# Two layers of a GLA, MLA and S5 hybrid: where S5 coefficients and powers are computed, how much filling goes where, and which PSUM banks GLA's decays use

## The chip, the cores and the metric

The kernel runs on one core of one Trainium2 chip. The metric is the device time of one execution in microseconds; the median of three runs is given. TensorE is called PE (PEld is its weight load), VectorE DVE, ScalarE ACT, GpSimd POOL; SP is the engine that issues the DMAs.

## The reference, cut to what matters

Two layers are computed for 512 latent tokens and 128 context tokens together (640 columns). Each layer normalises and modulates its input, projects it, runs three branches and merges them with sigmoid gates before an output projection:

```python
h = rms_norm(x, p['norm_w']) * (1.0 + scale) + shift
(gq, gk, gv, gaf, gab, g_gate, mq, mkv, mkr, m_gate, su, s_gate, merge) = split_cols(h @ p['w_in'], IN_SPLITS)
o_a = gla_mixer(...)      # gated linear attention, chunks of 64 tokens, both directions
o_b = mla_mixer(...)      # latent attention, 4 heads
o_c = s5_mixer(...)       # diagonal state space, both directions
g_a, g_b, g_c = jnp.split(jax.nn.sigmoid(merge), 3, axis=-1)
mixed = g_a * (o_a @ w_bo_gla) + g_b * (o_b @ w_bo_mla) + g_c * (o_c @ w_bo_s5)   # each o gated by silu
y = x + gate * (mixed @ p['w_out'])
```

Two pieces matter here. S5 needs coefficients that depend on weights alone (`s5_discretise`: exponentials, a sine and a cosine, a complex division) and the powers of the discretised transition; its linear scan is done in blocks. In GLA, each chunk of 64 tokens needs the cumulated decay `bcum`, from it three exponentials, and the addition `einsum('bhcd,bhce->bhde', kr, vi)` to the state that is carried from chunk to chunk.

## The kernel before, in words

**Layout and stages.** Activations stand with channels on partitions and the 640 tokens along the free axis. A projection takes 128 x 512 pieces of weights from DRAM (`raw`, tile `wraw`), splits each into a rounded high part on ACT (`whi`, line 227) and a remainder on DVE (`wlo`, line 236), and multiplies them with the split activations, all through one helper (line 245). Each layer goes in order through: the inputs of S5 (`s5_su`, `s5_kernel`, `s5_in`, `s5_z`), the S5 scan (`s5_pow`, `s5_scan`), S5's output (`s5_y`, `s5_gelu`), its gated linear unit (`s5_glu`), MLA (`mla_qkv`, `mla_heads`), GLA (`gla_in`, `gla_heads`), the last merge and the output projection.

**Filling.** The order of PE's instructions is the order in which the program writes them; all other engines are ordered by a scheduler with priorities (`high_priority`, a larger number is earlier) against a simulated timeline. Between its own steps a stage calls `fill(n)`, which takes n steps from a list of standing projections, `self.stand`: a step is one 128-row slice of a projection, six matmuls of 128 x 320. A projection from `h` has eight such steps. The list holds `mla_raw` (18 projections: S5 gates, MLA's latents, the output gates), then `mer_early` (8 merge gates, parked in DRAM), and after `s5_glu` also the merge of S5's branch. `settle` steps on to the end of the current projection; `fill(1000)` at the end of MLA drains what stands there. How many steps go where is set by `FILL` (S5, and MLA's inputs), `FM` (MLA's heads) and `FG` (GLA):

```python
FILL = (17, 2, 1, 4, 2, 10, 10, 1, 7, 3)
FM = (1, 6, 1, 4, 2, 4, 3, 2, 1)
```

`FILL[3]` is used after each of the 4 doublings of `s5_pow` and of the scan's steps, `FILL[4]` and `FILL[9]` in each of the four calls of `s5_y`, `FILL[5]` ahead of the gated linear unit.

**S5's coefficients.** `s5_prep` loads B and C (lines 636 to 641), and computes on DVE, in some 110 small instructions (lines 600 to 709), the powers `s5pw`, the weights `s5w` and the block transition `s5ab`. For layer 0 this is done at the start; for layer 1 by `s5_open(1)`, ahead of layer 0's last merge. `s5_kernel` then forms from them the tables `s5qk` (lines 716 to 718), and PE multiplies these in the course of layer 0's output projection.

**S5's powers.** `s5_pow` (lines 861 to 875) forms the powers 1 to 16 of the block transition (`s5pt`) by four doublings, just ahead of the scan that uses them (lines 896 to 934).

**PSUM.** The tiles `pj` (two of two banks) serve projections; four single banks (`bank`) serve all else. In `gla_head` the decays of a head are multiplied into two banks `pb` (the matmuls named `bank<-c,la`), and read by DVE (lines 1351, 1352) and ACT (`kd`, `eb`). The chunk additions (`bank<-gvt,krt`) go into four banks: chunk pair 4 into two, pairs 0 to 3 into two more; DVE reads pair 4 in lines 1403, 1404 and in the two `fin` updates of line 1400, and then the rest in the chain of `st` updates of the same line. `gla_heads` has the parts of neighbouring heads interleaved: the additions of head h are followed on PE by the decays of head h+1, then by eight steps of filling, then by the output of head h.

**Pools.** Tiles of a stage come from pools that are opened and closed like a stack; a tile that takes the place of another waits for the last use of that tile. `s5_in` and `s5_z` share one pool. The pools of MLA are opened right after the one of `s5_glu` is closed; MLA's keys `kt` are first written by ACT.

Of the kernel before, what the change touches and what calls it, by code (L numbers as in the profile page):

```python
# [10 lines left out]
F32 = mybir.dt.float32  # L11
# [8 lines left out]
L = 2  # L20
# [161 lines left out]
    return {k: np.ascontiguousarray(v) for k, v in r.items()}, at  # L182


FILL = (17, 2, 1, 4, 2, 10, 10, 1, 7, 3)
FM = (1, 6, 1, 4, 2, 4, 3, 2, 1)
FG = (8, 4, 8, 6)
TCARGS = dict(schedule_with_timeline_sim=True)
# [13 lines left out]
class Prog:  # L202
# [16 lines left out]
    def pool(self, name, bufs=1, **kw):  # L219
        return self.es.enter_context(self.tc.tile_pool(name=name, bufs=bufs, **kw))  # L220
# [95 lines left out]
    def consts(self):  # L316
        nc, a = self.nc, self.a
        c = self.cst.tile([128, 660], F32, name="c")
        self.S.dma_start(c, a["cst"])
        self.ident, self.trif, self.trib = (c[:, 128 * i:128 * i + 128] for i in range(3))  # L320
        self.eye16 = c[:, 384:400]
        self.rope = c[:, 400:656].rearrange("p (t r x) -> p t r x", t=4, r=2)
        self.sgn, self.nsgn, self.mhalf, self.one = (c[:, 656 + i:657 + i] for i in range(4))
        m = self.cst.tile([128, 2, 64], U32, name="msk")
        self.S.dma_start(m, a["msk"].rearrange("p (a b) -> p a b", a=2))
        self.msk = m
        cr, ct = (self.th.tile([128, NT], F32, name="tmp", tag="tmp", bufs=2)[:, 0:16].rearrange("p (a b) -> p a b", b=2)
                  for _ in range(2))
        self.S.dma_start(cr, a["cond"])
        self.act(ct, cr, AF.Tanh, scale=0.5)  # L330
        self.V.tensor_scalar(ct, ct, 0.5, 0.5, op0=ALU.mult, op1=ALU.add)
        cp = self.cst.tile([128, 8, 32], F32, name="cond")
        self.V.memset(cp, 0.0)
        self.V.tensor_tensor(cp[:, :, 0:2], ct, cr, op=ALU.mult)
        self.cond = cp
        self.kd = [self.dr.tile([16, 32, 240], F32, name=f"kd{l}") for l in range(L)]
        self.qd = [self.dr.tile([8, 2, 128, 512], F32, name=f"qd{l}") for l in range(L)]
        self.sud = [self.dr.tile([NT, 512], F32, name=f"sud{l}") for l in range(L)]
        self.gd = [self.dr.tile([8, 128, NT], F32, name=f"gd{l}") for l in range(L)]
        self.md = [self.dr.tile([8, 128, NT], F32, name=f"md{l}") for l in range(L)]  # L340
        self.x1 = self.dr.tile([8, 128, NT], F32, name="x1")

    def vecs(self, l):
# [285 lines left out]
        V.tensor_copy(e, k)  # L629
        V.tensor_tensor(out, y, e.bitcast(F32), op=ALU.mult)  # L630

    def s5_prep(self, l, vec, p, pz, ptmp):

        V = self.V
        n0 = VEC["B1"][0]
        bs, cs = pz.tile([128, 1024], F32, name="s5b"), p.tile([128, 1024], F32, name="s5c")
        with self.tc.high_priority(5200):
            for i, t in enumerate((bs, cs)):
                self.S.dma_start(t, self.a["vec"][l][:, n0 + 1024 * i:n0 + 1024 * i + 1024])
        self.B1, self.B2, self.C1, self.C2 = (t[:, 512 * i:512 * i + 512].rearrange("p (g c) -> p g c", c=16)  # L640
                                              for t in (bs, cs) for i in range(2))
        are, aim, ldt = vec("are"), vec("aim"), vec("ldt")
        sm = ptmp.tile([128, 11, 64], F32, name="s5sm")
        dt, tre, th, kk = (sm[:, i] for i in range(4))
# [29 lines left out]
        V.tensor_tensor(cs, c0, aq, op=ALU.mult)  # L674
        V.tensor_tensor(x2, s0, q, op=ALU.mult)
        V.tensor_tensor(cs, cs, x2, op=ALU.subtract)
        pw = p.tile([128, 9, 2, 64], F32, name="s5pw")
        V.memset(pw[:, 0, 0, :], 1.0)
        V.memset(pw[:, 0, 1, :], 0.0)
        V.tensor_tensor(pw[:, 1, 0], tre, cs, op=ALU.mult)  # L680
# [15 lines left out]
        e = lambda lo, hi, i: pw[:, lo:hi, i]  # L696
        for lo, hi, f in ((2, 3, 1), (3, 5, 2), (5, 9, 4)):
            n = hi - lo
            br, bi = (pw[:, f, i][:, None, :].to_broadcast([128, n, 64]) for i in range(2))
            self.cmul(V, ptmp, e(lo, hi, 0), e(lo, hi, 1), e(1, 1 + n, 0), e(1, 1 + n, 1), br, bi, [128, n, 64])  # L700
        w = pz.tile([128, 8, 2, 64], F32, name="s5w")
        br, bi = (t[:, None, :].to_broadcast([128, 8, 64]) for t in (cr, ci))
        self.cmul(V, ptmp, w[:, :, 0], w[:, :, 1], e(0, 8, 0), e(0, 8, 1), br, bi, [128, 8, 64])
        V.tensor_scalar(w[:, :, 1], w[:, :, 1], self.sgn, None, op0=ALU.mult)
        ab = p.tile([128, 2, 64], F32, name="s5ab")
        V.tensor_copy(ab[:, 0], pw[:, 8, 0])
        V.tensor_scalar(ab[:, 1], pw[:, 8, 1], self.nsgn, None, op0=ALU.mult)
        V.tensor_scalar(pw[:, 1:9, 0], pw[:, 1:9, 0], self.nsgn, None, op0=ALU.mult)
        V.tensor_scalar(pw[:, 1:9, 1], pw[:, 1:9, 1], -1.0, None, op0=ALU.mult)
        self.pw, self.w, self.ab = pw, w, ab  # L710

    def outer(self, eng, p, out, tmp, s1, s2, m1, m2, shape):

# [612 lines left out]
    def gla_head(self, p, h):  # L1326

        V, T, l = self.V, self.T, self.l
        v = self.gv
# [4 lines left out]
            self.copy(q[ds], self.gq[h // 2][hs])  # L1334
            self.copy(k[ds], self.gk[h // 2][hs])
        tri = (self.trif, self.trib)
        pb = [self.bank(), self.bank()]
        for t in range(5):
            for d in range(2):
                o = pb[t // 4][64 * d:64 * d + 64, 128 * (t % 4):128 * (t % 4) + 128]  # L1340
                self.mm(o, self.la[:, t, 128 * h + 64 * d:128 * h + 64 * d + 64], tri[d], tile_position=(0, 64 * d))
        big = lambda nm, b: p.tile([128, NT], F32, name=nm, tag=nm, bufs=b)
        eb, kd, kr = big("eb", 1), big("kd", 1), big("kr", 1)
        bl = p.tile([128, 10], F32, name="bl", tag="bl", bufs=2)
        for ps, c, n in ((pb[0], slice(0, 512), 8), (pb[1], slice(512, 640), 2)):
            src = ps[:, 0:64 * n]
            for d in range(2):
                s3 = src[64 * d:64 * d + 64].rearrange("p (c x) -> p c x", x=64)
                end = s3[:, :, 63:64] if d == 0 else s3[:, :, 0:1]
                e = bl[64 * d:64 * d + 64, c.start // 64:c.start // 64 + n]  # L1350
                V.tensor_copy(e, end[:, :, 0])
                V.tensor_tensor(kr[64 * d:64 * d + 64, c].rearrange("p (c x) -> p c x", x=64),
                                e[:, :, None].to_broadcast([64, n, 64]), s3, op=ALU.subtract)
            self.act(kd[:, c], src, AF.Exp, scale=-1.0)
            self.act(eb[:, c], src, AF.Exp)
# [8 lines left out]
        krt = p.tile([128, 5, 128], F32, name="krt", tag="krt", bufs=1)  # L1364
        for t0, nt in ((0, 4), (4, 1)):
            ps = self.bank()
# [5 lines left out]
        ps = [self.bank(), self.bank()]  # L1372
        for t in range(5):
            for d in range(2):
                for j in range(2):
                    c = slice(128 * t + 64 * j, 128 * t + 64 * j + 64)
                    self.mm(ps[d][64 * j:64 * j + 64, 64 * t:64 * t + 64], kd[64 * d:64 * d + 64, c], qd[64 * d:64 * d + 64, c],
                            tile_position=(64 * d, 64 * j))
# [8 lines left out]
        f, b = slice(0, 64), slice(64, 128)  # L1387
        self.S.dma_start(st[f, 0, :], self.a["sgla"][l, h, 0:64])
        self.S.dma_start(st[b, 7, :], self.a["sgla"][l, h, 64:128])
        pu = {}  # L1390
        for ts in ((4,), range(4)):
            ps = [self.bank(), self.bank()]
            for t in ts:
                for j in range(2):
                    r = slice(64 * j, 64 * j + 64)
                    pu[2 * t + j] = ps[j][:, 128 * (t % 4):128 * (t % 4) + 128]
                    self.mm(pu[2 * t + j], krt[r, t, :], v[r, t, 128 * h:128 * h + 128], tile_position=(64 * j, 0))

        def upd(r, out, c):
            V.scalar_tensor_tensor(out, st[r, c, :], bl[r, c:c + 1], pu[c][r], op0=ALU.mult, op1=ALU.add)  # L1400
# [12 lines left out]
        g = self.gate_in(4 + h)  # L1413
# [3 lines left out]
        ps = [self.bank(), self.bank()]  # L1417
        o = [ps[t // 4][:, 128 * (t % 4):128 * (t % 4) + 128] for t in range(5)]
# [18 lines left out]
        for t0, nt in ((0, 4), (4, 1)):  # L1437
            ps = self.bank()
            for t in range(t0, t0 + nt):
                T.transpose(ps[:, 128 * (t - t0):128 * (t - t0) + 128], on[:, t, :], self.ident)  # L1440
            c = slice(128 * t0, 128 * (t0 + nt))
# [24 lines left out]
    def fill(self, n):  # L1466

        for _ in range(n):
            while self.stand:
                try:  # L1470
                    next(self.stand[0])
                    break
                except StopIteration:
                    self.stand.pop(0)
# [14 lines left out]
    def s5_open(self, l):  # L1489

        es, ek = ExitStack(), ExitStack()
        pa = es.enter_context(self.pool_("s5a", l))
        pz = ek.enter_context(self.pool_("s5w", l))
        vec = self.nvec if l else self.vec
        with self.pool_("s5p", l) as p:
            self.s5_prep(l, vec, pa, pz, p)
        pk = ExitStack()
        self.s5 = es, ek, pk, pa, pz, self.s5_kernel(l, vec, pk.enter_context(self.pool_("s5k", l)))

    def layer(self, l, x):  # L1500
        tc = self.tc
        self.l = l
        self.layer_vecs()
        pool = lambda n, **kw: self.pool_(n, l, **kw)
        run = lambda g: [None for _ in g]
        step = lambda g, n: [next(g, None) for _ in range(n)]
        fill = self.fill
# [5 lines left out]
        if l == 0:  # L1513
# [8 lines left out]
            g = pair(0, 8000)  # L1522
            both(g, 2)
            n = self.h_rstd()
# [5 lines left out]
        else:  # L1530
            g = self.h_rstd()
# [9 lines left out]
        es, ek, pk, pa, pz, kern = self.s5  # L1541
# [24 lines left out]
            fill(2)  # L1566
        pk.close()
        self.late_vecs()
        with pool("s5i") as p, tc.high_priority(2000):
            self.s5_in(pa, p, fill)  # L1570
            self.s5_z(p, fill)
        ek.close()
        with ExitStack() as eg:
            with es:
                pq = es.enter_context(pool("s5q"))
                with pool("s5s") as p:
                    for _ in self.s5_pow(p):
                        fill(FILL[3])
                    for _ in self.s5_scan(p):
                        fill(FILL[3])  # L1580
                pg = eg.enter_context(pool("s5g", side="right"))
                gl = []
                with pool("s5y") as p:
                    for cb in range(4):
                        with tc.high_priority(2000):
                            y = self.s5_y(pq, p, cb, fill)
                        gl.append(self.s5_gelu(pg, y))
            with pool("s5b") as p:
                ogc = self.s5_glu(p, gl, self.gates, fill)
        self.stand = [g for g in self.stand if g is not early] + [  # L1590
            self.finish_tile(early), self.alternate(self.merge(2, ogc, 0), self.ada(l, self.vec, 2)), early]
# [62 lines left out]
```

## Time and profile before

| | |
|---|---|
| median of 3 runs | 1593.46 us (1589.63 to 1594.63) |
| the profiled execution | 1595.56 us, its span 1593.8 us |
| PE busy | 1517.0 us (95%) |
| DVE busy | 1051.9 us (66%) |
| ACT busy | 629.6 us (40%) |
| POOL busy | 48.0 us (3%) |
| TensorE clock granted, mean | 0.981 of full speed |

An engine is busy while one of its instructions runs. PE's busy time counts the whole length of matmuls that overlap, so what a matmul costs in a row of them is read from the distance of their starts. The chain of work that ended last follows the last instruction back through what released each step; PE has 87% of it. A granted clock below 1 in a stretch is a mean of the two levels 1.2 and 2.4 GHz.

### The profile page before, as it was taken

To read this page: it belongs to the slowest core of one execution; us is meant where nothing else is said; L and a number is where in the kernel's file an instruction comes from. 1 tells how busy PE (TensorE), PEld (TensorE's weight loads), DVE (VectorE), ACT (ScalarE), POOL (GpSimd) and SP (SyncE) were. 2 spreads that over 40 slices of the span, in tenths; PEclk is the share of its full clock that TensorE was granted. 3 is DMA by queue.
4 is the path that set the end of the run, shared out by engine and by line. 5 is a ranking of instruction groups with operands and counts; after the bars stand their busy time and mean duration, and the time that the engine had idled before them with its cause. 6 is when DMAs were issued, how large, how long until landed. Compare 5 with 4: busy or idle time off the path is not lost.

```text
span 1593.8 us, 28777 instructions
## 1 busy us (share of the span) xinstructions
PE 1517.0 (95%) x11334; PEld 1442.5 (91%) x11334; DVE 1051.9 (66%) x2435; ACT 629.6 (40%) x1171; POOL 48.0 (3%) x48
## 2 busy tenths in 40 slices
PE   5999999999999799999799999999999988999999
PEld 3789999999998688898797999999989988888998
DVE  8976993357666436879987579724766663487662
ACT  3335222545444355323223542244544443633331
POOL 0000000012000000000000000000210000000000
PEclk9999999999999899999999999999999999999999
DMA  9451435323321121227663432452333122222353
GB/s 348 156 150 50 142 122 155 119 86 113 116 61 52 46 76 52 68 90 242 216 202 90 124 113 90 130 160 77 100 119 95 62 66 66 64 65 62 93 168 106
DMA packets 108792, 179.73 MB, mean 113 GB/s; under 512 B 12656, under 2 KB 30768, under 8 KB 108656
## 3 DMA queue, kind: packets, MB, share of 16 engines
q1 hardware_dynamic: 108656, 177.89, 35.8%
q8 instruction: 89, 1.46, 0.4%
q14 instruction: 47, 0.39, 0.1%
HBM read 149.23 MB, written 28.61 MB: 112 GB/s over the span
## 4 chain that ended last, share of the span: by engine, by line
PE 87%; DVE 7%; DMA 3%; ACT 2%; issue 1%; SPq 0%; POOL 0%; DVEq 0%; ACTq 0%
PE pj L245 64%; PE bank L245 19%; PE bank L1236 2%; DMA wraw<-wpk 1%; PE bank L825 1%; DVE wlo L236 1%; ACT P L230 1%; DMA s5cr<-sud 1%; PE bank L1183 0%; DVE gt L418 0%; DVE smx L1211 0%; ACT whi L227 0%; DVE og L236 0%; DVE P L1222 0%; DVE mx L456 0%
## 5 line engine op out<-in xcount | busy, mean ns | idle before, releaser
L245 PE MATMUL pj<-h,whi 128*128 128x320 f32 x3456 | 662.8, 313 | 0.0
L245 PEld LDWEIGHTS pj<-h,whi 128*128 128x128 f32 x3456 | 541.2, 189 | 6.0 <-issue 5.1
L227 ACT ACTIVATE whi<-wraw 128x512 fp32r<-128x512 f32 x326 | 204.7, 631 | 502.0 <-PE pj L245 368.4
L245 PE MATMUL pj<-h,wlo 128*128 128x320 f32 x1728 | 397.4, 310 | 0.0
L236 DVE TENSOR_TENSOR wlo<-wraw,whi 128x512 fp32r<-128x512 f32 x326 | 223.5, 687 | 255.5 <-ACT whi L227 249.2
L245 PEld LDWEIGHTS pj<-h,wlo 128*128 128x128 f32 x1728 | 290.3, 188 | 0.0
L245 PE MATMUL pj<-og,whi 128*128 128x320 f32 x736 | 141.9, 313 | 1.0 <-DVE og L236 1.0
L245 PEld LDWEIGHTS pj<-og,whi 128*128 128x128 f32 x736 | 114.8, 188 | 5.0 <-issue 1.9
L245 PE MATMUL pj<-whi,h 128*128 128x512 f32 x256 | 87.0, 401 | 5.1 <-ACT h L230 4.4
L245 PE MATMUL pj<-og,wlo 128*128 128x320 f32 x384 | 87.5, 309 | 0.0
L245 PEld LDWEIGHTS pj<-whi,h 128*128 128x128 f32 x256 | 48.6, 192 | 18.3 <-ACT h L230 5.1
L245 PEld LDWEIGHTS pj<-og,wlo 128*128 128x128 f32 x384 | 64.2, 188 | 0.0
L230 ACT ACTIVATE P<-bank,smx 128x384 f32<-128x384 f32 x64 | 36.4, 575 | 56.3 <-DVE smx L1215 56.3
L236 DVE TENSOR_TENSOR Ptl<-bank,Pth 128x512 fp32r<-128x512 f32 x48 | 32.1, 688 | 35.5 <-ACT Pth L227 35.0
L230 ACT ACTIVATE th<-pj 128x640 f32<-128x640 f32 x72 | 49.7, 690 | 6.0 <-PE pj L245 6.0
L245 PE MATMUL pj<-wlo,h 128*128 128x512 f32 x128 | 50.7, 396 | 0.0
L245 PE MATMUL pj<-s5g,whi 128*128 128x320 f32 x256 | 49.2, 315 | 0.0
L245 PE MATMUL bank<-s5qy,mx 128*80 128x128 f32 x256 | 46.1, 302 | 0.0
L1236 PE MATMUL bank<-c,P 128*128 128x128 f32 x192 | 33.6, 315 | 12.8 <-ACT P L230 5.3
L227 ACT ACTIVATE Pth<-bank 128x512 fp32r<-128x512 f32 x48 | 27.5, 597 | 42.5 <-PE bank L1236 42.5
L1211 DVE TENSOR_REDUCE smx<-bank 128x1 f32<-128x384 f32 (+1 forms) x72 | 36.2, 523 | 9.4 <-PE bank L245 8.6
L245 PEld LDWEIGHTS pj<-s5g,whi 128*128 128x128 f32 x256 | 41.2, 193 | 0.0
(349 smaller groups left out, 2327.5 us busy)
## 6 DMA issues: line engine op xcount, KB each, us to landing
wraw<-wpk SPq DMA_DIRECT2D x358, 256.0 KB, 2.9
og<-wpk SPq DMA_DIRECT2D x48, 256.0 KB, 5.1
qd<-s5qk SPq DMA_DIRECT2D x32, 256.0 KB, 2.2
s5qy<-qd SPq DMA_DIRECT2D x32, 256.0 KB, 3.9
gd<-gt SPq DMA_DIRECT2D x16, 320.0 KB, 2.6
gt<-gd SPq DMA_DIRECT2D x16, 320.0 KB, 3.1
md<-th SPq DMA_DIRECT2D x16, 320.0 KB, 2.3
th<-md SPq DMA_DIRECT2D x16, 320.0 KB, 3.2
```

The source lines that it names most:

```text
L227: self.A.activation(out, in_, AF.Copy, scale=scale)
L230: self.A.activation(out, in_, f, **kw)
L236: (eng or self.V).tensor_tensor(lo, src, hi.bitcast(F32), op=ALU.subtract)
L245: self.T.matmul(out, lhsT, rhs, start=start, stop=stop, skip_group_check=True, **kw)
L825: self.T.transpose(ps[:, 128 * i:128 * i + 128], r[:, i].rearrange("p a b -> p (a b)"), self.ident)
L1211: V.tensor_reduce(mx[:, i:i + 1], ps[:, 0:w], axis=AX.X, op=ALU.max)
L1236: self.T.transpose(pt[:, nq * i + 128 * qi:nq * i + 128 * qi + 128], pr[qi][:, 128 * k:128 * k + 128], self.ident)
```

## The change

The diff, cut to its core:

```diff
-FILL = (17, 2, 1, 4, 2, 10, 10, 1, 7, 3)
+FILL = (17, 2, 1, 4, 1, 4, 10, 1, 7, 1)
+PREP = 200
+POW = 300
+        self.cd = self.dr.tile([128, 2304], F32, name="cd")
...
-    def s5_prep(self, l, vec, p, pz, ptmp):
+    def s5_prep(self, l, vec, p, pz):
...
+        self.pw = p.tile([128, 9, 2, 64], F32, name="s5pw")
+        self.w = pz.tile([128, 8, 2, 64], F32, name="s5w")
+        self.ab = p.tile([128, 2, 64], F32, name="s5ab")
+        if l:
+            for t, a, n in ((self.pw, 0, 9), (self.w, 1152, 8)):
+                self.S.dma_start(t, self.cd[:, a:a + 128 * n].rearrange("p (e r g) -> p e r g", r=2, g=64))
+            self.S.dma_start(self.ab, self.cd[:, 2176:2304].rearrange("p (r g) -> p r g", r=2))
+        else:
+            with self.pool_("s5p", l) as ptmp:
+                self.s5_coef(vec, self.pw, self.w, self.ab, ptmp)
+
+    def s5_coef_ahead(self, vec, p):
+        pw, w = p.tile([128, 9, 2, 64], F32, name="s5pw"), p.tile([128, 8, 2, 64], F32, name="s5w")
+        ab = p.tile([128, 2, 64], F32, name="s5ab")
+        self.s5_coef(vec, pw, w, ab, p)
+        for t, a, n in ((pw, 0, 9), (w, 1152, 8)):
+            self.S.dma_start(self.cd[:, a:a + 128 * n].rearrange("p (e r g) -> p e r g", r=2, g=64), t)
+        self.S.dma_start(self.cd[:, 2176:2304].rearrange("p (r g) -> p r g", r=2), ab)
+
+    def s5_coef(self, vec, pw, w, ab, ptmp):
...
-        pb = [self.bank(), self.bank()]
+        pb = self.rest if h else [self.bank(), self.bank()]
         for t in range(5):
             for d in range(2):
-                o = pb[t // 4][64 * d:64 * d + 64, 128 * (t % 4):128 * (t % 4) + 128]
+                o = pb[t // 3][64 * d:64 * d + 64, 128 * (t % 3):128 * (t % 3) + 128]
...
-        for ps, c, n in ((pb[0], slice(0, 512), 8), (pb[1], slice(512, 640), 2)):
+        for ps, c, n in ((pb[0], slice(0, 384), 6), (pb[1], slice(384, 640), 4)):
...
-        for ts in ((4,), range(4)):
-            ps = [self.bank(), self.bank()]
-            for t in ts:
-                for j in range(2):
-                    pu[2 * t + j] = ps[j][:, 128 * (t % 4):128 * (t % 4) + 128]
+        self.rest = [self.bank(), self.bank()]
+        ps = [self.bank(), self.bank()]
+        for t in (4, 0, 1, 2, 3):
+            for j in range(2):
+                pu[2 * t + j] = self.rest[j][:, 384:512] if t == 4 else ps[j][:, 128 * t:128 * t + 128]
...
-        with pool("s5i") as p, tc.high_priority(2000):
-            self.s5_in(pa, p, fill)
-            self.s5_z(p, fill)
+        with tc.high_priority(2000):
+            with pool("s5i") as p:
+                self.s5_in(pa, p, fill)
+            ep = ExitStack()
+            pt = ep.enter_context(pool("s5t", side="right"))
+            with tc.high_priority(-POW):
+                for _ in self.s5_pow(pt):
+                    pass
+            with pool("s5z") as p:
+                self.s5_z(p, fill)
...
                 with pool("s5s") as p:
-                    for _ in self.s5_pow(p):
-                        fill(FILL[3])
                     for _ in self.s5_scan(p):
                         fill(FILL[3])
+                ep.close()
...
-            with pool("s5b") as p:
+            with pool("s5b") as p, pool("s5f") as pf:
+                if l + 1 < L:
+                    with tc.high_priority(-PREP):
+                        self.s5_coef_ahead(self.nvec, pf)
                 ogc = self.s5_glu(p, gl, self.gates, fill)
```

So layer 1's coefficients are computed in layer 0 beside the gated linear unit, at a lowered priority, stored to DRAM (`cd`) and loaded again by `s5_open(1)`. The powers are written ahead of `s5_z`, with no filling between their doublings. `s5_y` gets 1 step of filling in each of two places where it had 2 and 3, the gated linear unit 4 where it had 10. In GLA, the additions of chunk pair 4 and the decays of the next head stand in the same two banks, in different columns.

## Rows read from the trace of the kernel before

**Rows 1.** Windows of 20 us: length, busy us (count) by engine, PE clock, DMA share, GB/s
```profile
340.00:360.00 20.00, 20.00 (x147) 19.16 (x146) 14.45 (x30) 11.75 (x23) 2.01 (x2) 1.00 0.36 105
...
520.00:540.00 20.00, 12.39 (x59) 10.56 (x60) 12.34 (x33) 8.83 (x24) 0.00 (x0) 0.73 0.06 23
...
780.00:800.00 20.00, 10.89 (x87) 10.25 (x86) 19.76 (x36) 3.75 (x6) 0.00 (x0) 0.80 0.55 187
```

**Rows 2.** Who waited for whom, PE: us in total, times, longest us
```profile
PE bank L245 <- DVE s5qk L718: 12.2, 4, 9.1
PE bank L245 <- DVE fin L1400: 9.0, 6, 2.1
```

**Rows 3.** The chain that ended last, by time: start us, us, what
```profile
160.52 100.35 PE pj L245 x684
260.87 6.21 PE bank L245 x48
...
303.84 17.64 PE pj L245 x120
```

**Rows 4.** Windows: the matmuls of `pj` alone in one MLA head
```profile
460.50:499.40 38.90, 28.43 (x177) 25.93 (x176) 1.64 (x2) 1.40 (x2) 1.00 0.21 63
```

**Rows 5.** PE's timeline: last filling in MLA's heads, first projection after them, both layers
```profile
501.71 0.75 PE L245 MATMUL pj<-h,whi 128*128 128x320 f32 x4
...
544.13 0.83 PE L245 MATMUL pj<-h,whi 128*128 128x320 f32 x4
...
1299.05 0.74 PE L245 MATMUL pj<-h,whi 128*128 128x320 f32 x4
...
1326.68 0.83 PE L245 MATMUL pj<-h,whi 128*128 128x320 f32 x4
```

**Rows 6.** Timeline of DVE and ACT: end of the scan; S5's output and its gelu
```profile
244.46 0.65 DVE L934 TENSOR_TENSOR mx<-mx,sf 128x480 f32<-128x480 f32 x1
...
267.12 0.59 ACT L227 ACTIVATE s5yb<-bank 80x512 f32<-80x512 f32 x1 [2.51 <-PE bank L245]
...
309.27 0.82 DVE L236 TENSOR_TENSOR s5g<-og,s5g 128x640 fp32r<-128x640 f32 x1 [0.30 <-ACT s5g L227]
```

**Rows 7.** ACT's last `s5cg`, and PE's first transposes of `s5_z`
```profile
123.26 1.06 ACT L227 ACTIVATE s5cg<-s5cr 80x1024 f32<-80x1024 f32 x1 [0.87 <-DMA s5cr<-sud]
...
124.98 0.60 PE L825 MATMUL bank<-c,s5r 128*128 128x128 f32 x4
```

**Rows 8.** Windows by tile: DVE's `ex`, `s5sm`, `cm` (coefficients), then `sp` (powers)
```profile
708.00:778.00 70.00, 8.63 (x44) 1.00 0.66 218
...
708.00:778.00 70.00, 12.32 (x61) 1.00 0.66 218
...
708.00:778.00 70.00, 9.09 (x24) 1.00 0.66 218
...
158.00:186.00 28.00, 9.10 (x24) 1.00 0.56 159
```

**Rows 9.** The chain that ended last, layer 0's output projection
```profile
796.59 2.69 PE bank L245 x26
799.28 8.63 PE pj L245 x48
807.91 1.47 PE bank L245 x26
```

**Rows 10.** Window of the gated linear unit, and ACT's first `kt`
```profile
303.84:323.61 19.77, 19.77 (x142) 19.77 (x141) 9.59 (x15) 10.22 (x17) 0.84 (x1) 1.00 0.32 102
...
354.39 0.38 ACT L227 ACTIVATE kt<-bank 128x256 f32<-128x256 f32 x1
```

**Rows 11.** GLA's timeline at one head change: DVE, PE, then ACT
```profile
618.29 0.72 DVE L1400 SCALAR_TENSOR_TENSOR fin<-st,bl,bank 64x128 f32<-64x128 f32 x2
...
618.77 1.31 PE L245 MATMUL bank<-c,la 128*64 128x128 f32 x20 [2.10 <-DVE fin L1400]
...
624.77 0.60 ACT L230 ACTIVATE kd<-bank 128x512 f32<-128x512 f32 x1 [8.99 <-DVE kr L1352]
```

More of the change, by code (lines that the diff above doesn't have):

```diff
@@ L630, in exp_ @@
         V.tensor_tensor(out, y, e.bitcast(F32), op=ALU.mult)
-    def s5_prep(self, l, vec, p, pz, ptmp):
-        V = self.V
+    def s5_prep(self, l, vec, p, pz):
         n0 = VEC["B1"][0]
@@ L641, in s5_prep @@
                                               for t in (bs, cs) for i in range(2))
+        self.pw = p.tile([128, 9, 2, 64], F32, name="s5pw")
[16 more added lines that the diff above has]
+    def s5_coef(self, vec, pw, w, ab, ptmp):
+        V = self.V
         are, aim, ldt = vec("are"), vec("aim"), vec("ldt")
@@ L676, in s5_prep @@
         V.tensor_tensor(cs, cs, x2, op=ALU.subtract)
-        pw = p.tile([128, 9, 2, 64], F32, name="s5pw")
         V.memset(pw[:, 0, 0, :], 1.0)
@@ L700, in s5_prep @@
             self.cmul(V, ptmp, e(lo, hi, 0), e(lo, hi, 1), e(1, 1 + n, 0), e(1, 1 + n, 1), br, bi, [128, n, 64])
-        w = pz.tile([128, 8, 2, 64], F32, name="s5w")
         br, bi = (t[:, None, :].to_broadcast([128, 8, 64]) for t in (cr, ci))
@@ L704, in s5_prep @@
         V.tensor_scalar(w[:, :, 1], w[:, :, 1], self.sgn, None, op0=ALU.mult)
-        ab = p.tile([128, 2, 64], F32, name="s5ab")
         V.tensor_copy(ab[:, 0], pw[:, 8, 0])
@@ L709, in s5_prep @@
         V.tensor_scalar(pw[:, 1:9, 1], pw[:, 1:9, 1], -1.0, None, op0=ALU.mult)
-        self.pw, self.w, self.ab = pw, w, ab
     def outer(self, eng, p, out, tmp, s1, s2, m1, m2, shape):
@@ L1390, in gla_head @@
         pu = {}
-        for ts in ((4,), range(4)):
-            ps = [self.bank(), self.bank()]
-            for t in ts:
-                for j in range(2):
-                    r = slice(64 * j, 64 * j + 64)
-                    pu[2 * t + j] = ps[j][:, 128 * (t % 4):128 * (t % 4) + 128]
-                    self.mm(pu[2 * t + j], krt[r, t, :], v[r, t, 128 * h:128 * h + 128], tile_position=(64 * j, 0))
+        self.rest = [self.bank(), self.bank()]
+        ps = [self.bank(), self.bank()]
+        for t in (4, 0, 1, 2, 3):
+            for j in range(2):
+                r = slice(64 * j, 64 * j + 64)
+                pu[2 * t + j] = self.rest[j][:, 384:512] if t == 4 else ps[j][:, 128 * t:128 * t + 128]
+                self.mm(pu[2 * t + j], krt[r, t, :], v[r, t, 128 * h:128 * h + 128], tile_position=(64 * j, 0))
         def upd(r, out, c):
@@ L1494, in s5_open @@
         vec = self.nvec if l else self.vec
-        with self.pool_("s5p", l) as p:
-            self.s5_prep(l, vec, pa, pz, p)
+        self.s5_prep(l, vec, pa, pz)
         pk = ExitStack()
```

## The prediction

> **What bounds the kernel now.** The table comes first: PE is busy for 1517.0 of 1593.8 us, so all that any reordering can win is the 77 us in which PE stands, and the time that it works at a lower clock. No matmul is removed. I therefore looked for the holes in PE with windows of 20 us: most are full, and some are not [rows 1]: 520 to 540 has PE busy for 12.39 us at a mean clock of 0.73 (part of it at 1.2 instead of 2.4 GHz), 780 to 800 for 10.89 us at 0.80. The list of PE's waits names what ends two kinds of hole: DVE's `s5qk` (12.2 us, one wait of 9.1) and `fin` (9.0 us in six waits) [rows 2]. The chain shows the opposite, stretches of S5 that are filling and nothing else: 100.35 us of `pj` beside the scan [rows 3]. The rest was read from timelines of those stretches.
>
> **Filling moved from S5 to MLA.** 684 matmuls in 100.35 us are 0.147 us each, so a step of six takes 0.88 us [rows 3]. Per layer 4 x 4 steps go from the powers, 4 x (1 + 2) from S5's output, 6 from ahead of the gated linear unit: 34. Ahead of that unit `settle` ends a projection: 120 matmuls stand there before, 20 steps, of which 8 are its own first projection and 10 `FILL[5]`, so 2 are `settle`'s [rows 3]; with 34 fewer it takes 4. Net 32 steps, 28.2 us, arrive in MLA.
>
> MLA runs out of them now. In layer 0 the last step starts at 501.71 and the next projection at 544.13; in layer 1 at 1299.05 and 1326.68 [rows 5]. From the ends of those steps that is 41.5 and 26.8 us. What PE must do there without filling: a full head takes 38.90 us with 177 matmuls of filling [rows 4], 26.0 us at 0.147, and the other 12.9 us hold by the code 101 matmuls, 0.128 each. Counted from the code, 142 such remain in layer 0 (from the second half of head 2's second score block) and 83 in layer 1 (in head 3): 18.2 and 10.6 us. So 23.3 and 16.2 us are latency and low clock. The steps that the code asks for in those stretches and does not get are 42 and 26, some 0.55 to 0.63 us lost for each. With 32 more, layer 1 is covered (16.2 us); layer 0 lacks 10, which keep about 6 us: 17.3 us. **Together -33.5 us**; none (0) if S5 turns out to need them all.
>
> Does S5 need them? The scan's last DVE instruction ends at 245.1 [rows 6], its first consumer on PE starts at 260.87 [rows 3]. 16 steps fewer bring that to 246.8; the powers, 24 small and medium instructions of 9.1 us together [rows 8], leave the scan too, so it ends at about 237. Covered, by 9 us. If the powers didn't fit ahead, cover would still be 1.6 us. In S5's output the last product of a block ends at 260.87 + 6.21 = 267.08, ACT's copy at 267.71 [rows 3, 6]; one step of 0.88 us covers all of it, a release may add some 0.2 us. Eight blocks: **+1.5 us**, between 0 and 8 x 2.64 = 21 (the three removed steps all idle). The gelu's last product is ready at 310.1 [rows 6], 6.3 us after the filling starts at 303.84 [rows 3]; the eight steps that stay last 7.0, and it is needed as the fourth slice, 2.6 us later. Covered.
>
> **Powers ahead of `s5_z`.** They run at a lower priority in DVE's idle time. The pool is split, so `s5_z`'s first tiles take the places of `s5cr` and `s5cg` and wait for their last uses. The last `s5cg` copy ends at 124.3; two DVE steps of 0.6 us each put the first transposes at about 125.6 in place of 124.98 [rows 7]: **+0.6 us a layer, +1.2**, between 0 and 4.
>
> **Layer 1's coefficients.** `ex`, `s5sm` and `cm` have 8.6, 12.3 and 9.1 us on DVE between 708 and 778 [rows 8]; some of it counts twice, 20 to 28 us is the load. DVE is full when PE waits 9.1 us for `s5qk` [rows 1, 2]. With that load gone, the tables (some 8 us for the first) are early and the wait goes. The 48 matmuls behind it took 8.63 us [rows 9] against 7.04 at 0.147: 1.6 us of low clock go with it. **-10.7 us**, or 0 if DVE's queue is still late. What is late next: the loads of the powers and weights, which the first table then waits for.
>
> Added: three stores to `cd` and three loads, 1.18 MB each way, on SP's queue. The loads fall in a stretch where DMA is at 0.55 to 0.66 of its time [rows 1, 8], with the weights' loads behind them: **+1 us**, 0 to 4. The computation itself lies beside the gated linear unit, where DVE is busy 9.59 of 19.77 us [rows 10] and then 14.45 of 20 [rows 1]: at these two rates 19 to 26 us are free until ACT writes the first `kt` at 354.39 [rows 10], about what the coefficients need. `kt` comes from a pool that takes over the place of the coefficients, so it waits for them and for the store; a few microseconds may show: **+2 us**, 0 to 8.
>
> **GLA's banks.** PE waits for `fin` ahead of the decays [rows 2, 11]: their new banks are those of chunk pair 4, free after DVE's reads. In the new form they are the same banks by construction, and other columns. If only columns counted, the 9.0 us would go. But ACT's `kd` stood 8.99 us until DVE's `kr` [rows 11]: neither reads what the other writes, they read one bank. I conclude that users of one bank are ordered whatever the columns, so the decays still stand behind `fin`, and behind the second one, since the first bank is the one that it reads: 0.72 / 2 = 0.36 us more for each of six [rows 11]: **+2.2 us**, between -9 and +2.2.
>
> The Trainium skill (PSUM — Partial Sum Buffer, on PSUM bank collisions) says that two engines must not use one bank in the same 32-partition quadrant at once, disjoint columns included, and that accesses are therefore serialised. By that rule the edit wins nothing, which the row of `kd` bears out; without it the sum would be 11 us lower.
>
> **The sum.** -33.5 + 1.5 + 1.2 - 10.7 + 1 + 2 + 2.2 = -36.3 us. From the profiled execution, 1595.56, that is 1559.3; it stands 2.1 us above the median of the runs, so I predict **1557 us**.
>
> **Rivals.** *S5 cannot spare its filling.* For: PE never waits there now, so its true slack is not seen, and each block's copy ends just when one step does. Against: the ends read above. All 21 us in place of 1.5: 1577.
>
> *DVE stays late at `s5qk`.* For: DVE has 19.76 of 20 us there [rows 1], some of it merge and projection work. Against: 20 us or more leave. 10.7 us come back: 1568.
>
> *Columns count in GLA*, and PE's decays go at once. Against: the `kd` row. 11 us less, and the state updates give a little back: 1547.
>
> *Slower: `kt` behind the coefficients.* Their lowered priority lets DVE's MLA work go first; then only about 5.5 of each 20 us are free [rows 1], and 25 us of work left over would stretch past 420. ACT is in order: with `kt` waiting, weight splits behind it stand, and PE with them. From 354 to past 400, less what PE has in hand, is 35 to 50 us, about 1597. It decides from 36 us on, where the whole gain is gone. Against: DVE is half idle for 40 us before, and the priority is lowered by 200 instructions only.
>
> **The numbers.** The forecast has 0.52, S5 short of filling 0.14, `s5qk` still late 0.12, columns in GLA 0.10, `kt` late 0.12. The range: the two nearer rivals and most of the first lie between 1545 and 1577, and the forecast's own unknowns (21, 4, 8, 4 us upwards, mostly not together) too; that leaves out the slow case and an edge of the others: 1543 to 1579. 0.3% (4.8 us) is about what a measurement of this kernel can tell from no change. Only the last rival reaches it: 0.05 within, 0.07 slower, 0.88 faster.
>
> **What would show it.** Right: no hole at 500 to 545 and 1300 to 1327 but for a short one in layer 0, head 3; the chain's stretch beside the scan near 86 us; no long wait on `s5qk`; `fin` still among PE's waits with about 9 to 11 us. Wrong: PE waiting for `s5yb`, for the scan or for `s5r` in S5; ACT's `kt` waiting for DVE or a store in layer 0; SP standing at a `cd` transfer while ACT waits for `wraw`; `fin` gone.

## The result and the profile after

The changed kernel takes **1575.01 us** (median of 6 runs, 1573.82 to 1577.47) against 1593.3 for the kernel before (6 runs): ratio 0.9892, 95% interval 0.9877 to 0.9906. It is 18.3 us faster by the medians, 17.2 by the ratio: inside the forecast range, with about half of the forecast gain of 36 us. The profiled execution takes 1574.24 us, its span is 1572.5 us, its mean granted clock 0.986 (0.981 before).

Windows of the changed kernel, columns as in [rows 1]:

```profile
120.00:140.00 20.00, 12.87 (x88) 12.36 (x87) 17.10 (x30) 7.26 (x14) 0.00 (x0) 0.74 0.18 57
...
340.00:360.00 20.00, 19.41 (x107) 17.10 (x108) 15.17 (x67) 9.67 (x20) 6.79 (x7) 0.91 0.32 103
520.00:540.00 20.00, 17.03 (x102) 15.77 (x100) 11.98 (x31) 8.73 (x20) 0.00 (x0) 0.83 0.25 77
720.00:740.00 20.00, 17.70 (x128) 14.76 (x129) 20.00 (x31) 4.64 (x8) 0.00 (x0) 1.00 0.91 293
780.00:800.00 20.00, 20.00 (x179) 19.27 (x178) 14.35 (x28) 5.65 (x10) 0.00 (x0) 1.00 0.57 193
880.00:900.00 20.00, 12.71 (x92) 12.27 (x90) 13.97 (x23) 8.09 (x15) 0.00 (x0) 0.83 0.16 44
1300.00:1320.00 20.00, 20.00 (x138) 20.00 (x137) 5.55 (x8) 6.21 (x10) 0.06 (x1) 1.00 0.38 119
```

The two holes of [rows 1] have moved. 780 to 800 is full, 520 to 540 has PE busy for 17.03 us in place of 12.39, and layer 1's MLA is full. Two new holes stand at 120 and 880, 7.1 and 7.3 us of idle PE, at 0.74 and 0.83 of the clock. They are in `s5_z` of the two layers. The list of PE's waits over the whole span names them (us in total, times, longest; lines of the helpers are two higher than before, `s5r` is line 738):

```profile
PE bank L845 <- DVE s5r L738: 11.4, 2, 6.1
PE bank L247 <- DVE fin L1421: 10.7, 6, 2.4
...
PE bank L247 <- DVE s5qk L738: 3.2, 3, 1.4
...
PE pj L247 <- DVE og L238: 2.4, 3, 1.4
PE bank L247 <- ACT kt L229: 2.4, 1, 2.4
```

Against [rows 2], `s5qk` fell from 12.2 to 3.2 us (what is left is layer 0's start), `fin` rose from 9.0 to 10.7, `og` from 1.0 to 2.4, and `s5r` is new. The wait for `og` lies at the last merge of layer 0, from 720 on, where DVE is busy for all of the 20 us.

PE's timeline at the last filling of MLA in layer 0, for [rows 5]:

```profile
528.83 0.75 PE L247 MATMUL pj<-h,whi 128*128 128x320 f32 x4
...
540.67 0.83 PE L247 MATMUL pj<-h,whi 128*128 128x320 f32 x4
```

11.8 us without filling are left where there were 42.4; layer 1 has none. The chain of the changed kernel reaches back over only 10% of its span (from 1421 us on), so nothing answers to [rows 3]. The 8.57, 12.45 and 9.00 us of `ex`, `s5sm` and `cm` on DVE [rows 8] now lie between 260 and 345.

The next three views show what happened ahead of `s5_z` in layer 0. DVE's timeline, kernel before:

```profile
102.45 0.69 DVE L716 TENSOR_TENSOR s5r<-s5w,s5b 128x512 f32<-128x512 f32 x1
...
107.27 1.29 DVE L718 TENSOR_TENSOR s5r<-s5r,s5rtmp 128x512 f32<-128x512 f32 x2
...
120.62 0.69 DVE L717 TENSOR_TENSOR s5rtmp<-s5w,s5b 128x512 f32<-128x512 f32 x1
```

DVE's timeline, changed kernel:

```profile
121.86 0.68 DVE L895 TENSOR_TENSOR s5pt<-sp,sp 128x512 f32<-128x512 f32 x1
...
126.65 0.69 DVE L736 TENSOR_TENSOR s5r<-s5w,s5b 128x512 f32<-128x512 f32 x1
...
130.86 1.28 DVE L738 TENSOR_TENSOR s5r<-s5r,s5rtmp 128x512 f32<-128x512 f32 x2
```

PE's timeline, changed kernel (last transposes of `s5_in`, first of `s5_z`):

```profile
125.54 0.87 PE L824 MATMUL bank<-c,s5cg 80*128 80x80 f32 x8 [1.84 <-ACT s5cg L229]
131.69 1.08 PE L845 MATMUL bank<-c,s5r 128*128 128x128 f32 x4 [5.29 <-DVE s5r L738]
```

Before, DVE starts on `s5r` at 102.45 and has several tables under way when PE comes to them at 124.98 [rows 7]. Now it starts at 126.65, a microsecond after PE's last `s5cg` transposes begin, runs seven multiplications first, and adds the first table at 130.86. PE begins 6.71 us later than before. Beside the wait the clock is low (0.74 of full speed from 120 to 140): the first four transposes of `s5r` last 1.08 us here, 0.60 before [rows 7].

To compare whole kernels I add two things over windows of 20 us: PE's idle time, and one minus the granted clock, times the length (the work that half clock would cost a PE that is busy throughout). In us, from one profiled execution each (for e6 its slowest, at 1572.48 us; for e3, e5 and e10 their fastest):

| stretch | before | after | e1 | e3 | e5 | e6 | e8 | e10 |
|---|---|---|---|---|---|---|---|---|
| 100-300, S5 of layer 0 | 0.7 | 12.6 | 1.8 | 0.4 | 0.5 | 2.3 | 0.2 | 0.6 |
| 300-420, inputs of MLA | 2.4 | 5.3 | 5.3 | 5.6 | 0.0 | 1.7 | 5.2 | 0.2 |
| 420-580, MLA of layer 0 | 21.6 | 6.8 | 5.4 | 7.0 | 19.7 | 7.0 | 0.4 | 9.9 |
| 680-860, to layer 1 | 18.8 | 4.7 | 9.2 | 4.5 | 6.0 | 22.4 | 8.8 | 6.7 |
| 860-1100, S5 of layer 1 | 1.2 | 10.7 | 1.4 | 2.7 | 1.4 | 3.4 | 1.4 | 2.8 |
| 1100-1340, MLA of layer 1 | 17.1 | 0.8 | 0.1 | 0.1 | 16.9 | 0.2 | 0.1 | 1.0 |
| whole span | 108.3 | 88.8 | 72.1 | 72.3 | 95.6 | 91.3 | 63.1 | 72.4 |

From before to after the sum falls by 19.5 us, the span by 21.3: nearly all of the result is in this table. The experiments behind the other columns follow.

### The profile page after: what moved, and what is told of

Its sections match the earlier page's. It is cut to its first block, busy times and chain, and to the rows that moved or that the text cites. A ratio compares the mean times of both kernels' runs of the same rounds, so it can differ in the third digit from the quotient of the medians.

```text
span 1572.5 us, 28798 instructions
## 1 busy us (share of the span) xinstructions
PE 1506.5 (96%) x11334; PEld 1436.7 (91%) x11334; DVE 1054.3 (67%) x2435; ACT 629.5 (40%) x1171; POOL 46.5 (3%) x48
## 5 line engine op out<-in xcount | busy, mean ns | idle before, releaser
L577 DVE SCALAR_TENSOR_TENSOR mx<-pj,ada,tmp 128x320 f32<-128x320 f32 (+2 forms) x48 | 18.1, 433 | 39.6 <-PE pj L247 37.5
L1421 DVE SCALAR_TENSOR_TENSOR st<-st,bl,bank 64x128 f32<-64x128 f32 x112 | 38.8, 347 | 3.5
```

What stands on the lines that cost most here:

```text
L577: V.scalar_tensor_tensor(xn[:, j, lo:hi], ps[:, i, lo - 320 * i:hi - 320 * i], self.ads[l, 2][r][:, j:j + 1], xr[:, lo:hi], op0=ALU.mult, ...
```

## The experiments

The theory: of the missing 18 us most are in `s5_z`, since the divided pool puts `s5r` and `s5rtmp` in the places of `s5cr` and `s5cg`. Rival A: the powers, now ahead on DVE, hold `s5r` back. Rival B: the loss lies elsewhere.

**e1, `s5r` (and with it `s5rtmp`) in a place of its own.** The powers stay written ahead.

```diff
+            pr = za.enter_context(pool("s5r"))
             with pool("s5i") as p:
                 self.s5_in(pa, p, fill)
...
             with pool("s5z") as p:
-                self.s5_z(p, fill)
+                self.s5_z(p, pr, fill)
...
-            r = p.tile([128, 4, 8, 16], F32, name="s5r", tag=f"s5r{d}", bufs=2 + d)
+            r = pr.tile([128, 4, 8, 16], F32, name="s5r", tag=f"s5r{d}", bufs=2 + d)
```

> The changed kernel, except that the tiles s5r and s5rtmp have a pool of their own that is opened ahead of s5_in, so that they no longer take the places of s5cr and s5cg; s5pm and the powers stay as in the changed kernel. Theory (the places hold s5r back): DVE again forms its first s5r products while the last blocks of s5_in are under way. PE's waits for s5r (11.4 us in two, 5.29 and 6.11) fall to under 2 us, and the windows 120:140 and about 880:900 (PE 12.87 us at a clock of 0.74, 12.71 at 0.83) are full again at 1.00. Idle time and low clock there are 12.3 and 10.7 us against 0.7 and 1.0 in the kernel before, so the time falls by 15 to 21 us, to about 1557. Rival A (the powers, ahead of s5_z on DVE, hold it back): they are still written ahead of it; the wait stays above 6 us and the time within 4 us of 1575. Rival B (the forecast's missing 18 us lie elsewhere, and what is won here is lost again behind it, in the scan or in S5's output): the s5r wait goes, a wait for the scan or for s5yb of about the same size comes, time above 1568.

Measured: 1561.67 us, ratio 0.9797 (0.9772 to 0.9823), some 15 us faster than the changed kernel. No wait for `s5r` is in the list; the windows of e1:

```profile
120.00:140.00 20.00, 19.82 (x164) 19.48 (x163) 17.24 (x41) 12.27 (x24) 0.00 (x0) 1.00 0.23 68
880.00:900.00 20.00, 18.59 (x157) 18.27 (x154) 15.79 (x37) 11.28 (x22) 0.00 (x0) 1.00 0.15 41
```

Both holes are filled, and no wait for the scan or for `s5yb` came in their place. The gain is at the lower end of what was expected. Rival B falls. DVE's timeline in e1:

```profile
102.89 0.69 DVE L736 TENSOR_TENSOR s5r<-s5w,s5b 128x512 f32<-128x512 f32 x1
...
125.34 0.29 DVE L881 COPY s5pt<-s5ab 128x64 f32<-128x64 f32 x2
```

With room for `s5r` the scheduler puts the powers behind the first tables, from 125.34 on; in the changed kernel they run from 102.08 to 122.5, while `s5r` has no place. So e1 doesn't settle rival A: the powers no longer run ahead in it. e2 does.

**e2, two pools, powers back in the scan.**

```diff
-            ep = ExitStack()
-            pt = ep.enter_context(pool("s5t", side="right"))
-            with tc.high_priority(-POW):
-                for _ in self.s5_pow(pt):
-                    pass
...
                 with pool("s5s") as p:
+                    for _ in self.s5_pow(p):
+                        pass
```

> The changed kernel with the powers back in the scan's pool (no filling between their doublings), but s5_in and s5_z still in two pools. Theory (the places): the wait for s5r stays at 11 us (10 to 13) although no power runs ahead of s5_z; the scan ends some 9 us later, which uses up about all of the 8.7 us by which PE's first s5qy product (254.71) now comes after the scan's end (246.0); time 1575 to 1585. Rival A (the powers): the wait for s5r falls to under 2 us.

Measured: 1572.59 us, ratio 0.9869 (0.9839 to 0.9900), the interval overlapping the changed kernel's. The wait in the list of e2:

```profile
PE bank L845 <- DVE s5r L738: 11.5, 2, 6.1
```

And DVE's timeline in e2:

```profile
119.75 0.69 DVE L238 TENSOR_TENSOR wlo<-wraw,whi 128x512 fp32r<-128x512 f32 x1 [2.70 <-ACT whi L229]
124.63 0.69 DVE L238 TENSOR_TENSOR wlo<-wraw,whi 128x512 fp32r<-128x512 f32 x1 [4.19 <-PE bank L824]
125.24 0.68 DVE L736 TENSOR_TENSOR s5r<-s5w,s5b 128x512 f32<-128x512 f32 x1
```

No power runs there, and DVE is busy for 5.99 of the 20 us from 100 to 120. Still `s5r` comes only at 125.24, behind a split for which DVE stood 4.19 us, put down to PE's transposes of `s5cg` (line 824). I read this as the scheduler's order: it has `s5r` late because the place is taken until then. In e3 below, which differs from e2 in the place alone, the first `s5r` starts at 102.66, as in e1 at 102.89. Rival A falls.

**e3, one pool, powers back in the scan.** This undoes the part as a whole: as e2, and

```diff
             with pool("s5i") as p:
                 self.s5_in(pa, p, fill)
-            with pool("s5z") as p:
                 self.s5_z(p, fill)
```

> The changed kernel with this part undone: s5_in and s5_z in one pool, the powers back in the scan's pool, without filling between their doublings. Theory: PE's waits for s5r fall to under 2 us as in the kernel before, worth 15 to 21 us; the scan ends about 9 us later than with the powers ahead, against a slack of 8.7 us in layer 0 and 11.8 in layer 1, so 0 to 3 us a layer are lost again: 1556 to 1564. Rival A expects the same fall; rival B expects 1568 or more. If S5 needs the powers ahead, a wait for mx of over 4 us a layer shows ahead of the first s5qy product.

Measured: 1562.25 us, ratio 0.9796 (0.9770 to 0.9822), the same as e1; no wait for `s5r`. In layer 0 the scan's last DVE instruction ends at 244.97 and PE's first product of `s5_y` starts at 245.59, without a wait for `mx`. So the part costs the change 0.0096 of 1593 us, 15 us, and the powers ahead of `s5_z` win nothing by themselves.

**e4, GLA's banks as before.**

```diff
-        pb = self.rest if h else [self.bank(), self.bank()]
+        pb = [self.bank(), self.bank()]
...
+        for ts in ((4,), range(4)):
+            ps = [self.bank(), self.bank()]
```

> The changed kernel with GLA's banks as before: two banks of their own for the decays, two for chunk pair 4. Theory: PE's waits for fin return from 10.7 us in six to about 9.0, and the time falls by 1 to 3 us, to 1572 to 1574. Rival (the shared banks win something that the list of waits doesn't show, in the state updates): 1 us or more slower than the changed kernel.

Measured: 1576.15 us, ratio 0.9887 (0.9858 to 0.9916). PE's wait for `fin` is 9.0 us again, as expected, but the time doesn't show it: the interval holds the changed kernel's 0.9892. In time the edit is not to be told from nothing.

**e5, all filling in its old place**, on e3: what is left of the change is layer 1's coefficients and GLA's banks.

```diff
-FILL = (17, 2, 1, 4, 1, 4, 10, 1, 7, 1)
+FILL = (17, 2, 1, 4, 2, 10, 10, 1, 7, 3)
...
                     for _ in self.s5_pow(p):
-                        pass
+                        fill(FILL[3])
```

> The kernel of the run before with the powers back (e3_pow_back), and all filling as in the kernel before, the steps between the doublings included: what is left of the change is layer 1's coefficients and GLA's banks. By the forecast's terms these are worth -10.7 + 1 + 2 + 2.2 = -5.5 us, so 1586 to 1590, and the filling, as the difference to e3_pow_back (1562.25), 32 us less what noise allows: 25 to 28 us here. PE is idle again in MLA's third or fourth head of both layers (about 12 and 9 us). Rival (the filling is worth 20 us or less, and the coefficients more than forecast): under 1582.

Measured: 1585.59 us, ratio 0.9936 (0.9921 to 0.9952). The holes in MLA are back in both layers (19.7 and 16.9 in the table). The filling is worth 0.9936 less 0.9796, 22 us, somewhat under the 25 to 28 that I expected here.

**e6, coefficients in their old place**, on e3.

```diff
-        if l:
-            for t, a, n in ((self.pw, 0, 9), (self.w, 1152, 8)):
...
-        else:
-            with self.pool_("s5p", l) as ptmp:
-                self.s5_coef(vec, self.pw, self.w, self.ab, ptmp)
+        with self.pool_("s5p", l) as ptmp:
+            self.s5_coef(vec, self.pw, self.w, self.ab, ptmp)
...
-                if l + 1 < L:
-                    with tc.high_priority(-PREP):
-                        self.s5_coef_ahead(self.nvec, pf)
```

> e3_pow_back with layer 1's coefficients computed where they were before, ahead of layer 0's last merge, no stores and loads of cd. By the forecast's terms -10.7 + 1 + 2 = -7.7 us go back: 1568 to 1572; PE waits for s5qk again, one wait of about 9 us, the wait for kt (2.5 us) is gone, and so are the 2.4 us for og at the third merge. Rival (the coefficients' wait was only a place where PE would have lost the time anyway): within 3 us of 1562.

Measured: 1564.25 us, ratio 0.9808 (0.9785 to 0.9831), only 2 us more than e3 where 6 to 10 were expected. The waits are as expected, 12.3 us for `s5qk` with 9.1 in one, no wait for `kt`, 1.0 us for `og`. The window of [rows 1] in e6:

```profile
780.00:800.00 20.00, 15.72 (x130) 14.98 (x131) 18.96 (x36) 3.37 (x6) 0.00 (x0) 0.74 0.57 203
```

The six executions lie between 1561.18 (clock 0.987) and 1572.48 (0.981), so the small difference is not settled. In idle PE alone e6's profiled execution, its slowest, has 61.0 us and e3's 52.5. And e5, which has the coefficients ahead and all filling in place, is 10 us faster than the kernel before, GLA's banks included. So the coefficients seem to be worth more with the filling in its old place than with it moved. By the medians this is at the edge of the noise; the table shows one place of it: the stretch from 300 to 420 loses 0.0 in e5, 1.7 in e6 and 5.6 in e3, where both are done.

**e10, ten steps ahead of the gated linear unit again**, on e3, to test that.

```diff
-FILL = (17, 2, 1, 4, 1, 4, 10, 1, 7, 1)
+FILL = (17, 2, 1, 4, 1, 10, 10, 1, 7, 1)
```

> e3_pow_back with ten steps of filling ahead of the gated linear unit again, in place of four; the rest of the filling stays moved. e5_old_fill, with all filling in its old place, shows no idle PE between 300 and 420, and e3_pow_back 3.8 us idle and 1.8 of low clock. Theory (kt's wait is bare only because the filling ahead of it was taken): the wait for kt (2.5 us) goes and that stretch is full, while MLA's heads in layer 0 lose up to six steps at some 0.6 us each; the time stays within 3 us of 1562. Rival (the wait for kt doesn't depend on the filling): it stays at 2 us or more and the time rises by 3 us or more.

Measured: ratio 0.9803 (0.9788 to 0.9818), the time of e3. Windows of e10:

```profile
320.00:340.00 20.00, 20.00 (x153) 18.56 (x151) 15.62 (x38) 13.30 (x26) 3.17 (x4) 1.00 0.47 150
500.00:520.00 20.00, 15.81 (x104) 14.58 (x102) 12.91 (x31) 10.01 (x24) 0.00 (x0) 1.00 0.25 80
520.00:540.00 20.00, 17.76 (x108) 16.77 (x108) 7.93 (x19) 7.00 (x16) 1.24 (x3) 0.83 0.25 66
```

The wait for `kt` is gone and 320 to 340 is full (17.55 us in e3, at 0.91), and MLA in layer 0 loses 2.9 us more; in time the two cancel. So these six steps cover the wait behind the computation ahead where they stand here, and a part of MLA where e3 has them: the two parts of the change share one cover, and each was priced as if it kept it.

**e7, the coefficients' pool on the other side**, on e3.

```diff
-            with pool("s5b") as p, pool("s5f") as pf:
+            with pool("s5b") as p, pool("s5f", side="right") as pf:
```

> e3_pow_back with the pool of the coefficients computed ahead (s5f) on the other side of the stack, so that MLA's kt need not take its place and wait for the store of s5pw to cd. Expected: PE's wait for kt (2.5 us) gone, with some low clock in 320 to 340 beside it; 2 to 4 us faster than e3_pow_back, 1558 to 1560. Rival (kt waits for DVE's own work in that stretch): the wait stays within 1 us, under another name or the same, and so does the time.

Measured: 1567.20 us, ratio 0.9822 (0.9805 to 0.9839), not faster. ACT's timeline in e7:

```profile
330.62 0.30 ACT L229 ACTIVATE kpe<-bank 128x160 f32<-128x160 f32 x1 [8.70 <-DMA cd<-s5w]
```

Now `kpe` lies in the place of a result that is still being stored; ACT stands 8.70 us, and PE waits 7.9 us for `cch` behind it. The prediction of a gain failed: moving the place only changes who waits.

**e8, the better version**: e1, GLA's banks as in e4, and eight steps fewer beside layer 0's scan.

```diff
-                    for _ in self.s5_scan(p):
-                        fill(FILL[3])
+                    for i, _ in enumerate(self.s5_scan(p)):
+                        fill(FILL[3] - (l == 0 and i < 8))
```

> e1_z_early (powers ahead, s5r in a place of its own), GLA's banks as before, and eight steps of filling fewer beside layer 0's scan, whose end lies 8.7 us ahead of its first use there (236.9 against 245.6). Theory: the eight steps, 7.0 us, arrive in MLA's fourth head of layer 0, where 3.5 us of PE's idle time and 1.8 of low clock are left, and fin gives 1.7 us: 1553 to 1557 from 1561.7. Rival (the scan is not covered any more, or MLA's latency is not filled by them): a wait for mx ahead of the first s5qy product or the same hole at 520 to 540, and 1559 or more.

Measured: **1553.17 us, ratio 0.9734 (0.9716 to 0.9753)**, 2.7% under the kernel before and 1.6% under the changed one. Windows of e8:

```profile
320.00:340.00 20.00, 16.76 (x100) 15.00 (x99) 16.25 (x67) 9.33 (x20) 6.99 (x7) 0.91 0.48 165
...
520.00:540.00 20.00, 19.63 (x137) 19.40 (x137) 6.29 (x10) 6.97 (x12) 1.24 (x3) 1.00 0.33 109
```

MLA in layer 0 loses 0.4 us where e1 lost 5.4. The scan ends at 236.22, PE's first product of `s5_y` starts at 237.90. What the powers ahead buy is slack in the scan: in e3 it ends at 244.97, so by these rows the same eight steps without the powers ahead would have left PE waiting some 7 us (an estimate; it was not run). e8 makes two edits at once; of the 9.0 us by which its sum in the table is below e1's, 5.0 are in layer 0's MLA, where the eight steps went.

**e9, results of the coefficients above their temporaries**, on e8.

```diff
-            with pool("s5b") as p, pool("s5f") as pf:
+            with pool("s5b") as p, pool("s5f") as pf, pool("s5h") as ph:
...
-                        self.s5_coef_ahead(self.nvec, pf)
+                        self.s5_coef_ahead(self.nvec, ph, pf)
```

> e8_best with the pool s5f divided in two: the temporaries of layer 1's coefficients below, the results that are stored to cd above, so that what follows in the lower place waits for DVE's last product (about 318 in e8_best) and not for the store of s5pw (issued at 319.0, 4.4 us). If kt's place is the lower one, PE's wait for kt (3.2 us, 1.8 of low clock beside it) goes, 3 to 5 us: 1548 to 1551. If another tile's turn comes at the store's place, or kt lies above, a wait of the same size stays and the time is within 2 us of 1553.

Measured: ratio 0.9746 (0.9733 to 0.9760), no gain; PE's wait for `kt` is still 2.8 us. ACT's timeline in e9:

```profile
323.25 0.63 ACT L229 ACTIVATE whi<-wraw 128x512 fp32r<-128x512 f32 x1 [1.81 <-DMA wraw<-wpk]
324.94 0.63 ACT L229 ACTIVATE whi<-wraw 128x512 fp32r<-128x512 f32 x1 [1.07 <-DMA wraw<-wpk]
...
325.84 0.65 ACT L229 ACTIVATE kt<-bank 128x256 f32<-128x256 f32 x2
```

The store isn't the last cause here: ACT runs two weight splits, which wait 1.81 and 1.07 us for their loads, ahead of `kt`, and `kt` then starts without a wait. ACT's timeline in the changed kernel, for [rows 10]:

```profile
337.75 0.63 ACT L229 ACTIVATE whi<-wraw 128x512 fp32r<-128x512 f32 x1 [1.55 <-DMA wraw<-wpk]
338.76 0.63 ACT L229 ACTIVATE whi<-wraw 128x512 fp32r<-128x512 f32 x1 [0.38 <-DMA wraw<-wpk]
...
340.15 0.66 ACT L229 ACTIVATE kt<-bank 128x256 f32<-128x256 f32 x2 [0.40 <-DMA cd<-s5pw]
```

The same splits stand ahead there, 1.55 and 0.38 us for loads, and then 0.40 for the store (1.23 in e8). The store and the splits end within 0.4 us of each other, so taking away one of the two wins 0.4 us at most. In e10, where PE doesn't wait for `kt`, ACT runs it at 331.15, ahead of both splits. Why the splits come first elsewhere, and why their loads come late, was not tried.

## Why the prediction was right or wrong

**The step that failed is the powers ahead of `s5_z`**: "two DVE steps of 0.6 us each put the first transposes at about 125.6 in place of 124.98 [rows 7]: **+0.6 us a layer, +1.2**, between 0 and 4". By the ratios of the changed kernel and e3 it costs 15 us, and e1 and e2 show that the place of `s5r` does it. I had seen that `s5_z`'s tiles would wait for the last uses of `s5cr` and `s5cg`, but took the tables to be made just in time, from PE's and ACT's rows at 123 to 125 [rows 7]. DVE's timeline from 102 to 121, which no term of the sum uses, shows a head start of some 20 us that the wait takes away. And a first table doesn't take two steps after the release: DVE's order was set for the head start, with seven multiplications ahead of the first addition, 126.65 to 130.86. The low clock beside PE's waits was not in the price either. This term alone is 14 of the 18 us between forecast and result. PE waiting for `s5r` was among the prediction's signs of being wrong, so the place was seen and its price was not.

By ratios the whole divides so: coefficients and GLA's banks won 10 us (e5) against 5.5 in the sum, the filling with S5's output 22 (e5 to e3) against 32, and the powers lost 15 (e3 to the changed kernel) against 1.2; each of these is known to some 3 to 5 us. The first two misses partly cancel, which is luck.

**Filling moved to MLA**: right in place and mechanism. Layer 1's MLA is covered as forecast (17.1 to 0.8 in the table, -16.3, against -16.2), layer 0's keeps a short hole (21.6 to 6.8, -14.8 against -17.3). By e3 and e5 it is 22 us of time against the 32 of -33.5 + 1.5. By the table, from e5 to e3, layer 1's MLA gains 16.8, layer 0's only 12.7 (17.3 in the sum), and the stretch from 300 to 420 loses 5.6, the cover taken from the coefficients. e8 bears out the price of a step: its eight steps took the loss in layer 0's MLA from 5.4 to 0.4, 0.63 us each, against the forecast 0.55 to 0.63.

**S5's output**: +1.5 us forecast, none seen; PE waits for nothing between 240 and 300. e3 also bears out the remark that cover would be left if the powers did not fit ahead: 0.6 us by its rows, against the forecast 1.6.

**Layer 1's coefficients**: right where the wait was; the stretch from 680 to 860 went from 18.8 to 4.7, more than the -10.7 + 1 of the sum, with the loads of `cd` and the 1.4 us more for `og` in it. In time the runs leave it open between 2 us (e6 to e3) and 10 (e5, with the banks). The cost at `kt`, +2, shows as a wait of 2.4 us and 2.9 us of loss from 300 to 420, but the reason given (place and store) is only part of it; e9 shows ACT's weight splits ahead of `kt`.

**GLA's banks**: right. `fin` went from 9.0 to 10.7 us in six waits, +1.7 against +2.2. The Trainium skill (PSUM — Partial Sum Buffer, on PSUM bank collisions) says that two engines must not use one bank in the same 32-partition quadrant at once, different columns included. By that rule the edit wins nothing; the list of waits agrees (10.7 us for `fin`, 9.0 in e4), and e4's time can't be told from the changed kernel's.

**The rivals.** S5 does not lack its filling; `s5qk` isn't late; columns don't count; `kt` is late by 2.4 us and not by 35 to 50. None of the four is what happened: the loss came from a term that I had bounded at 4 us.

## What to carry to other kernels

Where a pool is divided or a tile moved, look at how early the engine that writes it starts today, not at when the reader needs it: the head start is what a new place can take away, and an engine that is idle for 14 of 20 us, as DVE in e2, need not show that its work is waiting for room. Two edits that use the same filling as cover can't be priced one by one. Work computed ahead becomes time only once the slack it gives is spent: e1, with the powers ahead, takes the time of e3, without; e8, which has eight steps of filling fewer over that slack, is faster.

## What the runs showed that I had not expected

The same waits went with different clocks. In the changed kernel the 20 us from 600, with one 2.4 us wait for `fin`, have a granted clock of 1.00; in e1, with the same 2.4 us, 0.91. Six executions of e6 spread over 11 us at clocks of 0.981 to 0.988. So parts of some 2 us, such as GLA's banks or what is left at `kt`, are read from idle time in the profile rather than from medians.
